# Down projection: three of eight seven-product weight sums per group formed by adding DMAs

## The chip, the core and the metric

One core of one Trainium2 chip runs the kernel. The metric is the device time of one execution in microseconds. Before the change it is 1316.98 us, the median of two runs (1316.85 and 1317.11).

The engines are called as in the profile: PE is TensorE (PEld its weight loads), DVE is VectorE, ACT is ScalarE, POOL is GpSimd, and SP is the engine that only issues transfers here.

## The reference

A block of an encoder with 256 positions of 2048 features in float32: RMSNorm, a combined input projection, a gated branch and a neighbourhood attention, a gated merge, an output projection; then the channel mixer, and a last RMSNorm. The change is in the channel mixer's down projection, `x + a @ w_down`, in which `a` has 256 x 5504 elements and `w_down` 5504 x 2048:

```
h = rms_norm(x, g_norm)
up = h @ w_up
up = (pad[:, :t] * conv_k[0] + pad[:, 1:t + 1] * conv_k[1]
      + pad[:, 2:t + 2] * conv_k[2] + conv_b)
gate, val = jnp.split(up, 2, axis=-1)
return x + (jax.nn.silu(gate) * val) @ w_down
```

## The kernel before

Every float32 operand of a matmul is split in two float32r parts, high and low, and a product is a triple of matmuls: high by high, low by high, high by low (`triple`, L291 to L293). ScalarE makes the high part (L151) and VectorE the low one (L152).

The down projection runs as two groups, each for 1024 output columns. A group walks over the 43 blocks of 128 rows of `w_down`. One such block of 128 x 1024 is a piece: a transfer of 512 KB into one of five raw buffers `wraw` (L126), issued by SP, then the split into `whi` and `wlo`. For a plain piece four triples are multiplied: two blocks of positions (t) by two halves of columns (c). Two pieces make a pair, numbered from 0, so pair q has the pieces 2q and 2q + 1.

In some pairs (`DOWN_QUADS`, seven per group before) the two by two by two block product is done with seven triples in place of eight, with sums of activation blocks and sums of weight blocks (a scheme of the Strassen and Winograd kind). Three helpers prepare such a pair:

- `act_sums` and `act_sums_split` (L295 to L311): one DVE addition of 128 x 512 joins high and low (L298), four of 128 x 128 make the sums (L300 to L303), ACT and DVE split them again (L309, L310).
- `weight_sums` (L313 to L320): four DVE instructions of 128 x 512 on the raw pieces (L316 to L319) make two tiles of 128 x 2 x 512, `t13` and `t24`.
- `weight_sums_split` (L322 to L330): for each of the two tiles an ACT copy (L326) and a DVE subtraction (L327) of 128 x 1024.

The order of all engines is the order of the program, written out by hand: each piece i has a `begin(i)`, which issues loads up to piece i + 4 (`LOAD_AHEAD`), splits pieces up to i + 3 (`SPLIT_AHEAD`), and runs the tasks that were put `at(i)`. For a pair that starts at piece i the activation sums stand at i - 5 and i - 4, the weight sums at i - 3, their split at i - 2. In the products (`run_wide`) the first piece of the pair brings three triples, on raw blocks and one activation sum; the second brings four, on the weight sums.

Each engine takes its instructions in this order. A transfer that SP issues waits on SP's queue until its buffer is free, and holds those behind it. The same is true of POOL's queue, which has few transfers in this stage: the four loads of the last norm's weights (`gfin`, L1272).

Of the kernel before, what the change touches and what calls it, by code (L numbers as in the profile page):

```python
# [8 lines left out]
F32 = mybir.dt.float32  # L9
F32R = mybir.dt.float32r  # L10
AF = mybir.ActivationFunctionType
OP = mybir.AluOpType
# [43 lines left out]
OUT_ORDER = (tuple(range(16)), (0, 1, 6, 7, 2, 3, 10, 11, 4, 5, 8, 9, 12, 13, 14, 15))  # L56
TURN_X2 = (13, 1)
Y_GAP = 224
DOWN_QUADS = ((4, 6, 9, 11, 14, 16, 18), (3, 5, 8, 10, 13, 15, 17))


@with_exitstack
def trunk_kernel(ctx, tc, x, norm_mix, w_in, ln_g, ln_b, w_s, b_s, rpb, w_branch, w_out,
# [41 lines left out]

    raw, split_t = {}, {}
    whole, units = {}, {}
    n_loaded = [0]
    n_split = [0]
    first = {}  # L110

    def load_to(n):
        while n_loaded[0] < min(n, len(pieces)):
            i = n_loaded[0]
            n_loaded[0] += 1
            if i in preload:
                for f in preload[i]:
                    f()
            src, r0, kn, (c0, cn, nb, cs), step = pieces[i]
            w = wpool.tile([128, 2, 512], F32, name="wraw", bufs=LOAD_AHEAD)  # L120
            ld = src.shape[-1]
            if i == 0:
                for k in range(kn):
                    nc.sync.dma_start(w[:, k, :cn], src[r0:r0 + 128, c0 + k * step:c0 + k * step + cn])
            elif nb == 1:
                nc.sync.dma_start(  # L126
                    w[:, :kn, :cn],
                    bass.AP(tensor=src.tensor, offset=src.offset + r0 * ld + c0,
                            ap=[[ld, 128], [step, kn], [1, cn]]))
            else:  # L130
                for b in range(nb):
                    nc.sync.dma_start(
                        w[:, :kn, b * cn:(b + 1) * cn],
                        bass.AP(tensor=src.tensor, offset=src.offset + r0 * ld + c0 + b * cs,
                                ap=[[ld, 128], [step, kn], [1, cn]]))
            raw[i] = w
            if i in whole:
                whole[i] = w
# [30 lines left out]
    def at(i, f):  # L169
        tasks.setdefault(i, []).append(f)  # L170
# [93 lines left out]

    def wide(src, row0, order, c0, acts, quads, room, done, sums=None, odd=None):
        n0 = plan_wide(src, row0, order, c0)
        boxes = {}
        for n, q in enumerate(quads):  # L270
            i = n0 + 2 * q
            own = odd if odd and n % 2 else room
            whole[i] = whole[i + 1] = None
            units[i], units[i + 1] = 1, 2
            b = boxes[q] = {}
            if sums is None:
                b["acts"] = {}
                sum_acts_at(i - 5, i - 4, b["acts"], lambda k=order[2 * q]: ff["ap"][k // 2], room, "s")
            else:
                b["acts"] = sums[order[2 * q]]  # L280
            at(i - 3, lambda i=i, b=b: weight_sums(i, b, room))
            at(i - 2, lambda b=b, own=own: weight_sums_split(b, own))
        return ("wide", n0, order, acts, quads, boxes, done)

# [10 lines left out]
    def act_sums(a, box, room):  # L295
        w = room("f", F32)
        f = w[:, 0].rearrange("p (k t) -> p k t", k=2)
        nc.vector.tensor_add(f, a[:, :, 0, :].bitcast(F32), a[:, :, 1, :].bitcast(F32))  # L298
        s1, s2, s3, s4 = (w[:, 1, n * 128:(n + 1) * 128] for n in range(4))
        nc.vector.tensor_add(s1, f[:, 0, 128:], f[:, 1, 128:])  # L300
        nc.vector.tensor_sub(s3, f[:, 0, :128], f[:, 0, 128:])
        nc.vector.tensor_sub(s2, s1, f[:, 0, :128])
        nc.vector.tensor_sub(s4, f[:, 1, :128], s2)  # L303
        box["w"] = w

    def act_sums_split(box, room, name):
# [6 lines left out]
    def weight_sums(i, box, room):  # L313
        r0, r1 = whole.pop(i), whole.pop(i + 1)
        t13, t24 = room("t13", F32), room("t24", F32)
        nc.vector.tensor_sub(t13[:, 0], r0[:, 1], r0[:, 0])  # L316
        nc.vector.tensor_sub(t24[:, 0], r1[:, 1], t13[:, 0])
        nc.vector.tensor_sub(t13[:, 1], r1[:, 1], r0[:, 1])
        nc.vector.tensor_sub(t24[:, 1], r1[:, 0], t24[:, 0])  # L319
        box["w"] = (t13, t24)  # L320

    def weight_sums_split(box, room):  # L322
        u = []
        for name, t in zip(("13", "24"), box.pop("w")):
            h, l = room("h" + name, F32R), room("l" + name, F32R)
            nc.scalar.activation(h, t, AF.Copy)  # L326
            nc.vector.tensor_sub(l, t, h.bitcast(F32))  # L327
            u.append((h, l))
        box["t"] = {1: [x[:, 0] for x in u[0]], 3: [x[:, 1] for x in u[0]],
                    2: [x[:, 0] for x in u[1]], 4: [x[:, 1] for x in u[1]]}  # L330

    def run_wide(g, tail=0):
        kind, n0, order, acts, quads, boxes, done = g
        n1 = n0 + len(order)
        P = C = None

        def x_of(k, t):
            a = acts(k)
            return a[:, 0, t * 128:(t + 1) * 128], a[:, 1, t * 128:(t + 1) * 128]

        def plain(i, t, c):
            h, l = split_t[i]
            triple(C[t][c], x_of(order[i - n0], t), h[:, c], l[:, c], i == n0, i == n1 - 1)

        for i in range(n0, n1 - tail):
            begin(i)
            q, r = divmod(i - n0, 2)
            if C is None:
                c = [bank() for _ in range(4)]
                C = [c[:2], c[2:]]  # L350
            if q not in quads:
                for t, c in ((0, 0), (0, 1), (1, 0), (1, 1)) if i > 1 else ((0, 0), (1, 0), (0, 1), (1, 1)):
                    plain(i, t, c)
                split_t.pop(i)
                continue
            st, sp = q == quads[0], q == quads[-1]
            k, k1 = order[2 * q:2 * q + 2]
            if r == 0:
                if st:
                    P = [bank() for _ in range(4)]  # L360
                (h0, l0), (h1, l1) = split_t[i], split_t[i + 1]
                triple(P[0], x_of(k, 0), h0[:, 0], l0[:, 0], st, sp)
                triple(C[0][0], x_of(k1, 0), h1[:, 0], l1[:, 0], False, False)
                triple(C[0][1], boxes[q]["acts"]["s"][3], h1[:, 1], l1[:, 1], False, False)
                split_t.pop(i)
                split_t.pop(i + 1)
                continue
            S, W = boxes[q]["acts"]["s"], boxes[q]["t"]
            triple(P[1], S[0], *W[1], st, sp)
            triple(P[3], S[2], *W[3], st, sp)  # L370
            triple(P[2], S[1], *W[2], st, sp)
            triple(C[1][0], x_of(k1, 1), *W[4], False, False)
            if sp:
                done[0](P, i)
        if not tail:
            done[1](C, n1)
            return
        for t in range(NT):
            for c in range(2):
                for i in range(n1 - tail, n1):  # L380
                    if t == 0 and c == 0:
                        begin(i)
                    plain(i, t, c)
                done[1](C, t, c)
# [140 lines left out]
    def post_sums(P, x, spare):  # L525
        p1, p5, p6, p7 = P
        (x11, x12), (x21, x22) = x
        nc.scalar.activation(x11, p1, AF.Copy)
        nc.vector.tensor_add(spare, p6, x11)
        nc.vector.tensor_add(x12, p5, spare)  # L530
        nc.vector.tensor_add(x21, p7, spare)
        nc.vector.tensor_add(x22, p5, x21)

    def add_sums(ps, x):
        for t in range(NT):
            for c in range(2):
                nc.vector.tensor_add(x[t][c], ps[t][c], x[t][c])

    def ev_v_sums(P, i):
        def go():  # L540
# [358 lines left out]
    def ev_sums(j, room):  # L899
        def done(P, i):  # L900
# [5 lines left out]
            def first_half():  # L906
# [1 line left out]
                m["v"], m["u3"], m["w"] = cd[:, 0], cd[:, 1], ab[:, 0]  # L908
                nc.scalar.activation(ab[:, 0], p1, AF.Copy)
                nc.vector.tensor_add(x11, p1, x11)  # L910
                nc.vector.tensor_add(ab[:, 1], p6, ab[:, 0])
                nc.vector.tensor_add(m["v"], p5, ab[:, 1])
                nc.vector.tensor_add(m["u3"], p7, ab[:, 1])
                nc.vector.tensor_add(m["w"], p5, m["u3"])

            def second_half():
                nc.vector.tensor_add(x12, x12, m["v"])
                nc.vector.tensor_add(x21, x21, m["u3"])
                nc.vector.tensor_add(x22, x22, m["w"])

            at(i + 1, first_half)
            at(i + 2, second_half)
# [48 lines left out]
    ff = {}  # L971
# [166 lines left out]
    def down_room(name, dt):  # L1138
        return hpool.tile([128, 2, 512], dt, name=h_room[name])

    g_dn = [wide(w_d, 0, range(NF), g * 1024, lambda k: ff["a"][k], DOWN_QUADS[g], down_room,
                 (ev_sums(2 * g, down_room), ev_down if g == 0 else finish)) for g in range(2)]


    preload[0] = [lambda: load_x(0, 256)]
# [103 lines left out]
    ctx.push(fa_st)  # L1249
    ff["ap"] = [fa.tile([128, min(2, NF - k), 2, T], F32R, name=f"a{k // 2}") for k in range(0, NF, 2)]  # L1250
    ff["a"] = [ff["ap"][k // 2][:, k % 2] for k in range(NF)]
    fc = {}

    def open_conv():
# [54 lines left out]
```

## Time and profile before

| | us |
|---|---|
| median of the two runs | 1316.98 |
| span of the profiled execution | 1314.9 |
| TensorE busy | 1303.3 |
| VectorE busy | 1066.2 |
| ScalarE busy | 764.8 |
| GpSimd busy | 88.3 |
| DMA read from HBM | 253.90 MB, 195 GB/s over the span |

The runs' median lies 2.08 us above the profiled execution's span; the profile lists no other time of that execution. Rows of the order of time read: start, length, engine, line, operation, tiles written and read, shapes, count; behind them in brackets the idle time before and what ended it. In rows of groups the last numbers are the busy time, the mean length of one in ns, and the idle time before. The first group of the down projection begins at about 1080 us and the second at about 1193 us. The tiles of the sums are all named `h` in the profile, since they live in buffers of that name.

### The profile page before, as it was taken

To read this page: it belongs to the slowest core of one execution; us is meant where nothing else is said; L and a number is where in the kernel's file an instruction comes from. 1 tells how busy PE (TensorE), PEld (TensorE's weight loads), DVE (VectorE), ACT (ScalarE), POOL (GpSimd) and SP (SyncE) were. 2 spreads that over 40 slices of the span, in tenths; PEclk is the share of its full clock that TensorE was granted. 3 is DMA by queue.
4 is the path that set the end of the run, shared out by engine and by line. 5 is a ranking of instruction groups with operands and counts; after the bars stand their busy time and mean duration, and the time that the engine had idled before them with its cause. 6 is when DMAs were issued, how large, how long until landed. Compare 5 with 4: busy or idle time off the path is not lost.

```text
span 1314.9 us, 19329 instructions
## 1 busy us (share of the span) xinstructions
PE 1303.3 (99%) x6776; PEld 1112.0 (85%) x6776; DVE 1066.2 (81%) x1625; ACT 764.8 (58%) x1139; POOL 88.3 (7%) x176
## 2 busy tenths in 40 slices
PE   9999999999999999999999999999999999999997
PEld 7888888888888888888888888888888888888885
DVE  7996778667789966986777778787878789999997
ACT  5766476666645644556555555555656556555653
POOL 0004505323000000000000000000000000000000
PEclk9999999999999999999999999999999999999999
DMA  8768656556556657665565665656565656666663
GB/s 305 260 209 235 201 174 201 181 163 194 179 172 209 210 190 241 204 210 163 175 202 182 192 193 182 195 184 193 180 205 177 198 154 226 220 194 206 210 202 119
DMA packets 170577, 259.37 MB, mean 197 GB/s; under 512 B 12664, under 2 KB 124144, under 8 KB 170480
## 3 DMA queue, kind: packets, MB, share of 16 engines
q1 hardware_dynamic: 166448, 250.31, 59.4%
q0 software_dynamic: 3712, 7.30, 2.4%
q8 instruction: 53, 0.87, 0.3%
q10 hardware_dynamic: 320, 0.53, 0.1%
q14 instruction: 44, 0.36, 0.1%
HBM read 253.90 MB, written 2.10 MB: 195 GB/s over the span
## 4 chain that ended last, share of the span: by engine, by line
PE 97%; DVE 1%; ACT 0%; issue 0%; DMA 0%; ACTq 0%; DVEq 0%
PE bank L205 31%; PE bank L209 16%; PE bank L293 12%; PE bank L291 12%; PE bank L292 12%; PE bank L233 5%; PE bank L235 4%; PE bank L234 4%; PE bank L761 1%; DVE wlo L152 0%; PE bank L811 0%; PE bank L503 0%; PE bank L627 0%; PE bank L801 0%; PE bank L892 0%
## 5 line engine op out<-in xcount | busy, mean ns | idle before, releaser
L152 DVE TENSOR_TENSOR wlo<-wraw,whi 128x1024 fp32r<-128x1024 f32 (+1 forms) x472 | 550.3, 1178 | 188.7 <-ACT whi L151 92.0
L151 ACT ACTIVATE whi<-wraw 128x1024 fp32r<-128x1024 f32 (+1 forms) x472 | 472.0, 1015 | 204.7 <-PE bank L292 75.2
L205 PE MATMUL bank<-h,whi 128*128 128x512 f32 x1760 | 426.0, 392 | 0.0
L205 PEld LDWEIGHTS bank<-h,whi 128*128 128x128 f32 x1760 | 321.9, 188 | 62.0 <-DVE ya L631 0.3
L209 PEld LDWEIGHTS bank<-h,wlo 128*128 128x128 f32 x1760 | 225.9, 191 | 8.8
L209 PE MATMUL bank<-h,wlo 128*128 128x256 f32 x1760 | 228.6, 283 | 0.0
L989 ACT ACTIVATE tc<-ta,ck 128x256 f32<-128x256 f32 x86 | 47.1, 594 | 117.1 <-DVE ta L987 117.1
L293 PE MATMUL bank<-wlo,a 128*128 128x512 f32 x260 | 101.5, 390 | 0.2 <-DVE wlo L152 0.2
L292 PE MATMUL bank<-whi,a 128*128 128x512 f32 x260 | 101.2, 389 | 0.0
L291 PE MATMUL bank<-whi,a 128*128 128x512 f32 x260 | 101.2, 389 | 0.0
L291 PE MATMUL bank<-whi,h 128*128 128x512 f32 x204 | 80.3, 393 | 0.0
L292 PE MATMUL bank<-whi,h 128*128 128x512 f32 x204 | 79.5, 390 | 0.0
L293 PE MATMUL bank<-wlo,h 128*128 128x512 f32 x204 | 79.5, 390 | 0.0
L293 PEld LDWEIGHTS bank<-wlo,a 128*128 128x128 f32 x260 | 48.8, 188 | 11.2 <-DVE wlo L152 1.3
L292 PEld LDWEIGHTS bank<-whi,a 128*128 128x128 f32 x260 | 48.8, 188 | 10.3
L291 PEld LDWEIGHTS bank<-whi,a 128*128 128x128 f32 x260 | 48.8, 188 | 10.1
L992 DVE SCALAR_TENSOR_TENSOR tc<-ta,ck,tc 128x255 f32<-128x255 f32 x86 | 41.4, 481 | 14.5 <-ACT tc L989 14.5
L979 ACT ACTIVATE tb<-bank 128x256 f32<-128x256 f32 x86 | 28.3, 385 | 42.2 <-PE bank L205 42.2
L233 PE MATMUL bank<-whi,y 128*128 128x512 f32 x128 | 50.5, 394 | 0.0
L233 PE MATMUL bank<-whi,h 128*128 128x512 f32 x128 | 50.4, 394 | 0.0
L235 PE MATMUL bank<-wlo,h 128*128 128x512 f32 x128 | 49.9, 390 | 0.0
L235 PE MATMUL bank<-wlo,y 128*128 128x512 f32 x128 | 49.9, 390 | 0.0
(299 smaller groups left out, 1744.1 us busy)
## 6 DMA issues: line engine op xcount, KB each, us to landing
wraw<-in_w_up_dram SPq DMA_DIRECT2D x336, 256.0 KB, 3.2
wraw<-in_w_in_dram SPq DMA_DIRECT2D x111, 512.0 KB, 4.5
wraw<-in_w_down_dram SPq DMA_DIRECT2D x86, 512.0 KB, 4.6
wraw<-in_w_in_dram SPq DMA_DIRECT2D x66, 256.0 KB, 3.2
wraw<-in_w_branch_dram SPq DMA_DIRECT2D x32, 512.0 KB, 4.5
wraw<-in_w_out_dram SPq DMA_DIRECT2D x32, 512.0 KB, 3.6
xs<-in_x_dram SPq DMA_DIRECT2D x8, 256.0 KB, 7.6
vw<-y POOLq DMA_DIRECT2D x16, 128.0 KB, 6.9
```

Of the source, the lines that this page charges most:

```text
L151: nc.scalar.activation(h[:, k, :m], w[:, k, :m], AF.Copy)
L152: nc.vector.tensor_sub(l[:, k, :m], w[:, k, :m], h[:, k, :m].bitcast(F32))
L205: nc.tensor.matmul(p, h[:, k - k0, b * 128:(b + 1) * 128], acts(k), start=k == 0, stop=k == nk - 1)
L209: nc.tensor.matmul(p[:, :T], l[:, k - k0, b * 128:(b + 1) * 128], acts(k)[:, 0, :], start=False, stop=False)
L233: nc.tensor.matmul(p, xh, h[:, kk, :m], start=st, stop=False)
L234: nc.tensor.matmul(p, xl, h[:, kk, :m], start=False, stop=False)
L235: nc.tensor.matmul(p, xh, l[:, kk, :m], start=False, stop=sp)
L291: nc.tensor.matmul(p, xh, h, start=st, stop=False)
L292: nc.tensor.matmul(p, xl, h, start=False, stop=False)
L293: nc.tensor.matmul(p, xh, l, start=False, stop=sp)
L989: nc.scalar.activation(v, u, AF.Identity, scale=ck[:, 1, ch:ch + 1], bias=ck[:, 3, ch:ch + 1])
L992: nc.vector.scalar_tensor_tensor(v[:, 1:], u[:, :T - 1], ck[:, 0, ch:ch + 1], v[:, 1:], op0=OP.mult, op1=OP.add)
```

## The change

It does five things.

- The seven-product scheme is written in another form, so that the four weight sums are additions only. This touches the order of the products, the signs in the combinations after them, and the activation sums, which become four DVE instructions in place of five. It holds for all stages that use the scheme.
- Each group of the down projection has eight seven-product pairs in place of seven.
- In three of the eight (pairs 6, 10, 14 of the first group and 5, 9, 13 of the second) the weight sums are not made by VectorE. SP loads `t13` and `t24` straight from `w_down`, and POOL issues three transfers that add to their destination: a second load added to `t13`, half of one added to `t24`, then the first half of `t13` added to both halves of `t24`. They stand at i - 7.
- For such a pair only the first half of piece i is loaded raw.
- `t13` and `t24` of these pairs live in a pool of their own, with one buffer each. The ring memory for POOL's transfers is set to 4096 bytes.

```diff
-DOWN_QUADS = ((4, 6, 9, 11, 14, 16, 18), (3, 5, 8, 10, 13, 15, 17))
+DOWN_QUADS = ((4, 6, 8, 10, 12, 14, 16, 18), (3, 5, 7, 9, 11, 13, 15, 17))
+DOWN_BY_DMA = ((6, 10, 14), (5, 9, 13))
...
+            if i in first_half:
+                kn = 1
...
+            if q in by_dma:
+                at(i - 7, lambda i=i, b=b: weight_sums_dma(i, b, dma_room))
+            else:
+                at(i - 3, lambda i=i, b=b: weight_sums(i, b, room))
             at(i - 2, lambda b=b, own=own: weight_sums_split(b, own))
...
-        nc.vector.tensor_add(s1, f[:, 0, 128:], f[:, 1, 128:])
-        nc.vector.tensor_sub(s3, f[:, 0, :128], f[:, 0, 128:])
-        nc.vector.tensor_sub(s2, s1, f[:, 0, :128])
-        nc.vector.tensor_sub(s4, f[:, 1, :128], s2)
+        nc.vector.tensor_sub(w[:, 1, 0:256].rearrange("p (n t) -> p n t", t=128), blocks[:, 0:4:3],
+                             blocks[:, 1:2].to_broadcast([128, 2, 128]))
+        nc.vector.tensor_add(p2, n1, a11)
+        nc.vector.tensor_sub(s4, a12, p2)
...
-        nc.vector.tensor_sub(t13[:, 0], r0[:, 1], r0[:, 0])
-        nc.vector.tensor_sub(t24[:, 0], r1[:, 1], t13[:, 0])
-        nc.vector.tensor_sub(t13[:, 1], r1[:, 1], r0[:, 1])
-        nc.vector.tensor_sub(t24[:, 1], r1[:, 0], t24[:, 0])
+        nc.vector.tensor_add(t13[:, 0], r0[:, 0], r0[:, 1])
+        nc.vector.tensor_add(t24[:, 1], t13[:, 0], r1[:, 1])
+        nc.vector.tensor_add(t13[:, 1], r0[:, 1], r1[:, 1])
+        nc.vector.tensor_add(t24[:, 0], r1[:, 0], t24[:, 1])
...
+        def part(dr, c, step, n=2):
+            return bass.AP(tensor=src.tensor, offset=src.offset + (r0 + dr) * ld + c0 + c,
+                           ap=[[ld, 128], [step, n], [1, 512]])
+
+        nc.sync.dma_start(t13, part(0, 0, 512))
+        nc.sync.dma_start(t24, part(128, 0, 512))
+        nc.gpsimd.dma_start(t13, part(0, 512, 128 * ld), accum_op=OP.add)
+        nc.gpsimd.dma_start(t24[:, 0:1], part(128, 512, 512, 1), accum_op=OP.add)
+        nc.gpsimd.dma_start(t24, t13[:, 0:1].to_broadcast([128, 2, 512]), accum_op=OP.add)
...
-            triple(P[1], S[0], *W[1], st, sp)
-            triple(P[3], S[2], *W[3], st, sp)
-            triple(P[2], S[1], *W[2], st, sp)
+            triple(P[1], S[1], *W[1], st, sp)
+            triple(P[3], S[0], *W[3], st, sp)
+            triple(P[2], S[2], *W[2], st, sp)
...
-            nc.vector.tensor_add(spare, p6, x11)
+            nc.vector.tensor_sub(spare, x11, p6)
...
-    nc = _bacc.Bacc("TRN2", target_bir_lowering=False, num_devices=1)
+    nc = _bacc.Bacc("TRN2", target_bir_lowering=False, num_devices=1, dynamic_dma_scratch_size=4096)
```

More of the change, by code (lines that the diff above doesn't have):

```diff
@@ L107, in trunk_kernel @@
     whole, units = {}, {}
+    first_half = set()
     n_loaded = [0]
@@ L262, in run_group, with wide @@
             done(ps, b)
-    def wide(src, row0, order, c0, acts, quads, room, done, sums=None, odd=None):
+    def wide(src, row0, order, c0, acts, quads, room, done, sums=None, odd=None, by_dma=(), dma_room=None):
         n0 = plan_wide(src, row0, order, c0)
@@ L272, in wide @@
             own = odd if odd and n % 2 else room
-            whole[i] = whole[i + 1] = None
             units[i], units[i + 1] = 1, 2
+            if q in by_dma:
+                first_half.add(i)
+            else:
+                whole[i] = whole[i + 1] = None
             b = boxes[q] = {}
@@ L280, in wide @@
                 b["acts"] = sums[order[2 * q]]
-            at(i - 3, lambda i=i, b=b: weight_sums(i, b, room))
+            if q in by_dma:
+                at(i - 7, lambda i=i, b=b: weight_sums_dma(i, b, dma_room))
+            else:
+                at(i - 3, lambda i=i, b=b: weight_sums(i, b, room))
             at(i - 2, lambda b=b, own=own: weight_sums_split(b, own))
@@ L298, in act_sums @@
         nc.vector.tensor_add(f, a[:, :, 0, :].bitcast(F32), a[:, :, 1, :].bitcast(F32))
-        s1, s2, s3, s4 = (w[:, 1, n * 128:(n + 1) * 128] for n in range(4))
-        nc.vector.tensor_add(s1, f[:, 0, 128:], f[:, 1, 128:])
-        nc.vector.tensor_sub(s3, f[:, 0, :128], f[:, 0, 128:])
-        nc.vector.tensor_sub(s2, s1, f[:, 0, :128])
-        nc.vector.tensor_sub(s4, f[:, 1, :128], s2)
+        a11, a21, a12, a22 = (w[:, 0, n * 128:(n + 1) * 128] for n in range(4))
+        blocks = w[:, 0].rearrange("p (n t) -> p n t", t=128)
+        nc.vector.tensor_sub(w[:, 1, 0:256].rearrange("p (n t) -> p n t", t=128), blocks[:, 0:4:3],
+                             blocks[:, 1:2].to_broadcast([128, 2, 128]))
+        n1, p2, s4 = (w[:, 1, n * 128:(n + 1) * 128] for n in range(1, 4))
+        nc.vector.tensor_add(p2, n1, a11)
+        nc.vector.tensor_sub(s4, a12, p2)
         box["w"] = w
@@ L315, in weight_sums, with weight_sums_dma @@
         t13, t24 = room("t13", F32), room("t24", F32)
-        nc.vector.tensor_sub(t13[:, 0], r0[:, 1], r0[:, 0])
-        nc.vector.tensor_sub(t24[:, 0], r1[:, 1], t13[:, 0])
-        nc.vector.tensor_sub(t13[:, 1], r1[:, 1], r0[:, 1])
-        nc.vector.tensor_sub(t24[:, 1], r1[:, 0], t24[:, 0])
+        nc.vector.tensor_add(t13[:, 0], r0[:, 0], r0[:, 1])
+        nc.vector.tensor_add(t24[:, 1], t13[:, 0], r1[:, 1])
+        nc.vector.tensor_add(t13[:, 1], r0[:, 1], r1[:, 1])
+        nc.vector.tensor_add(t24[:, 0], r1[:, 0], t24[:, 1])
+        box["w"] = (t13, t24)
+    def weight_sums_dma(i, box, room):
+        src, r0, _, (c0, _, _, _), _ = pieces[i]
+        ld = src.shape[-1]
+        t13, t24 = room("t13", F32), room("t24", F32)
+        def part(dr, c, step, n=2):
[6 more added lines that the diff above has]
+        nc.gpsimd.dma_start(t24, t13[:, 0:1].to_broadcast([128, 2, 512]), accum_op=OP.add)
         box["w"] = (t13, t24)
@@ L329, in weight_sums_split @@
         box["t"] = {1: [x[:, 0] for x in u[0]], 3: [x[:, 1] for x in u[0]],
-                    2: [x[:, 0] for x in u[1]], 4: [x[:, 1] for x in u[1]]}
+                    2: [x[:, 1] for x in u[1]], 4: [x[:, 0] for x in u[1]]}
     def run_wide(g, tail=0):
@@ L536, in add_sums @@
             for c in range(2):
-                nc.vector.tensor_add(x[t][c], ps[t][c], x[t][c])
+                (nc.vector.tensor_sub if c else nc.vector.tensor_add)(x[t][c], ps[t][c], x[t][c])
     def ev_v_sums(P, i):
@@ L910, in first_half @@
                 nc.vector.tensor_add(x11, p1, x11)
-                nc.vector.tensor_add(ab[:, 1], p6, ab[:, 0])
+                nc.vector.tensor_sub(ab[:, 1], ab[:, 0], p6)
                 nc.vector.tensor_add(m["v"], p5, ab[:, 1])
@@ L916, in second_half @@
             def second_half():
-                nc.vector.tensor_add(x12, x12, m["v"])
+                nc.vector.tensor_sub(x12, x12, m["v"])
                 nc.vector.tensor_add(x21, x21, m["u3"])
-                nc.vector.tensor_add(x22, x22, m["w"])
+                nc.vector.tensor_sub(x22, x22, m["w"])
             at(i + 1, first_half)
@@ L1139, in down_room, with more_room @@
         return hpool.tile([128, 2, 512], dt, name=h_room[name])
+    def more_room(name, dt):
+        return ff["more"].tile([128, 2, 512], dt, name=name)
     g_dn = [wide(w_d, 0, range(NF), g * 1024, lambda k: ff["a"][k], DOWN_QUADS[g], down_room,
-                 (ev_sums(2 * g, down_room), ev_down if g == 0 else finish)) for g in range(2)]
+                 (ev_sums(2 * g, down_room), ev_down if g == 0 else finish), by_dma=DOWN_BY_DMA[g], dma_room=more_room)
+            for g in range(2)]
     preload[0] = [lambda: load_x(0, 256)]
@@ L1251, in trunk_kernel @@
     ff["a"] = [ff["ap"][k // 2][:, k % 2] for k in range(NF)]
+    ff["more"], more_st = pool("more")
+    ctx.push(more_st)
     fc = {}
```

## The prediction

> **What bounds the kernel now.** I read the page's first part and its chain first, then busy time by stretch for the down projection, then who made TensorE wait, then the order of time on TensorE, VectorE and the load queue around the pairs that the change touches.
>
> ```profile
> span 1314.9 us, 19329 instructions
> PE 1303.3 (99%) x6776; PEld 1112.0 (85%) x6776; DVE 1066.2 (81%) x1625; ACT 764.8 (58%) x1139; POOL 88.3 (7%) x176
> PE 97%; DVE 1%; ACT 0%; issue 0%; DMA 0%; ACTq 0%; DVEq 0%
> ```
> ```profile
> 1100.00:1176.00 76.00, 76.00 (x337) 62.94 (x336) 73.31 (x104) 42.98 (x49) 0.00 (x0) 1.00 0.62 205
> ```
> ```profile
> PE bank L291 <- ACT h L326: 0.6, 1, 0.6
> PE bank L293 <- DVE wlo L152: 0.2, 1, 0.2
> ```
>
> TensorE is busy for 1303.3 of 1314.9 us and carries 97% of the chain. In the seven-product part of the first down group (second fence, columns PE, PEld, DVE, ACT, POOL, clock, DMA share, GB/s) it never stops, the clock is full, and VectorE works 73.31 of 76 us. In the whole span it waits 0.8 us for ScalarE and VectorE after its start (third fence). So every matmul removed is time won, as long as nothing else begins to arrive late; and VectorE has little room for another pair's sums.
>
> The median of the two runs is 1316.98 us, 2.08 above the profiled span. I carry these 2.08 us along unchanged.
>
> **The change part by part.**
>
> *One more seven-product pair in each group.* It drops one product, three matmuls, per group. The first matmuls that use the sums of pairs 4 and 18 of the first group:
>
> ```profile
> 1104.31 0.39 PE L291 MATMUL bank<-h,h 128*128 128x512 f32 x1
> ...
> 1176.39 0.39 PE L291 MATMUL bank<-h,h 128*128 128x512 f32 x1
> ```
>
> Between them lie 6 seven-product pairs of 21 matmuls and 8 plain ones of 24, 318 in 72.08 us, so 0.2267 us each (the 0.39 is one matmul's own duration; they overlap). Six fewer: 1.36 us, all on the path.
>
> *VectorE.* Here is one full seven-product pair and the plain pair behind it:
>
> ```profile
> 1093.67 0.68 DVE L298 TENSOR_TENSOR h<-a 128x512 f32<-128x512 f32 x1
> ...
> 1095.33 0.42 DVE L486 TENSOR_TENSOR a<-tc,a 128x256 fp32r<-128x256 f32 x1
> 1095.66 1.22 DVE L152 TENSOR_TENSOR wlo<-wraw,whi 128x1024 fp32r<-128x1024 f32 x1
> ...
> 1098.00 0.69 DVE L316 TENSOR_TENSOR h<-wraw 128x512 f32<-128x512 f32 x1
> ...
> 1100.54 1.22 DVE L152 TENSOR_TENSOR wlo<-wraw,whi 128x1024 fp32r<-128x1024 f32 x1
> ...
> 1105.08 0.68 DVE L298 TENSOR_TENSOR h<-a 128x512 f32<-128x512 f32 x1
> ```
>
> From one L298 to the next are 11.41 us, of which 0.33 (L486) belong to the stage before: 11.08 us of VectorE against 45 x 0.2267 = 10.20 of TensorE. That is why before has room for two dense pairs and then needs a longer gap. The four weight sums take 1100.54 - 1098.00 = 2.54 us, so a pair whose sums come by DMA costs 8.54 with its plain neighbour. Alternating, the mean is 9.81, under 10.20: VectorE gains room although there are more pairs.
>
> ```profile
> L301 DVE TENSOR_TENSOR h<-h 128x128 f32<-128x128 f32 x14 | 4.0, 285 | 0.0
> ```
>
> The activation sums lose one instruction (five to four; two of 128x128 become one of 128x256), between nothing and 0.29 us for each set, off the path, in all stages. The sign changes in the combinations swap one addition for one subtraction of the same shape: nothing. Half of one raw piece per DMA pair is no longer loaded; loads are no bound. ScalarE gets the operand splits of one more pair per group, under 4 us, at 42.98 busy of 76.
>
> *The DMA chain.* For each of six pairs SP issues two 512 KB loads, and POOL three adding transfers: A (512 KB into t13), B (256 KB into t24), C (512 KB, t13 into both halves of t24). A waits for t13's load, C for A and B. ScalarE's L326 and VectorE's L327 then split the results. In the changed kernel's instruction order the two loads stand right behind the load of the group's piece i-3, for pair 6 piece 9. Counted back from the load that had to wait for the weight sums of piece 8, that is the row at 1088.24.
>
> ```profile
> 1088.24 0.33 SPq L126 DMA_DIRECT2D wraw<-in_w_down_dram  x1
> ```
> ```profile
> 1115.87 0.39 PE L291 MATMUL bank<-h,h 128*128 128x512 f32 x1
> ...
> 1131.51 0.39 PE L291 MATMUL bank<-h,h 128*128 128x512 f32 x1
> ```
> ```profile
> 1126.09 2.36 DVE L327 TENSOR_TENSOR h<-h,h 128x1024 fp32r<-128x1024 f32 x2
> ```
> ```profile
> L327 DVE TENSOR_TENSOR h<-h,h 128x1024 fp32r<-128x1024 f32 x28 | 32.9, 1218 | 0.0
> L326 ACT ACTIVATE h<-h 128x1024 fp32r<-128x1024 f32 x28 | 28.2, 1054 | 21.3 <-DVE h L318 21.2
> wraw<-in_w_down_dram SPq DMA_DIRECT2D x86, 512.0 KB, 4.6
> ```
>
> Pair 6 stands at the same place in both kernels, and TensorE first uses a product of t24 there at 1115.87. Less 1.22 (L327) and 1.05 (L326), t24 must be complete at 1113.60. The load goes out at 1088.57: 25.0 us, less 4.6 for the load, leave 20.4 us for A + B + C, where B counts only what it adds behind A.
>
> The later DMA pairs have less. t13 and t24 have one buffer each, so the next load waits for the previous pair's L327, and two DMA pairs stand 90 matmuls, 20.4 us, apart. VectorE can be ahead of the need: pair 9 of before had its L327s done at 1128.45, 3.06 before 1131.51. Over the two gaps of a group that makes 21.9 us each. The t13 load may start 1.13 (one L327's step) before the second L327 ends; then 4.6 for the load, A + B + C, 1.05 and 1.22. So A + B + C may take 16.2 us; beyond that everything is late by the difference, in pairs 10 and 14, then 9 and 13.
>
> No row shows an adding transfer. The nearest are plain ones from POOL's queue: four of 512 KB issued together, and two of 256 KB by themselves.
>
> ```profile
> L927 POOL DMA_DIRECT2D x<-in_x_dram x4: 704/711/728, 512.7 to 514.8; - x4
> DMA to landing us min/median/max: 6.4/7.8/10.4
> ```
> ```profile
> L1272 POOL DMA_DIRECT2D gfin<-in_norm_final_dram x2: 537/538/539, 1210.1 to 1214.1; - x2
> DMA to landing us min/median/max: 3.6/4.0/4.4
> ```
>
> Taking the shortest as the first and the longest as the last, the four landed between 519.1 and 525.2: 2.0 us for each further 512 KB, 1.0 for 256. So A and C lie between 3.6 + 1.0 = 4.6 and 10.4. I take 6.4, the first of the four, as the row of the same queue, size and source beside the same kind of loads, and 1.0 for B: 13.8 us, 2.4 less than the later pairs allow.
>
> Does the volume fit? Each 20.4 us gain 1.05 MB of loads less 0.26 (39 GB/s) and 1.31 MB of adds (64, or 128 if each byte counts twice), on 205: 308 to 372 GB/s. The core has moved more:
>
> ```profile
> 16.00:20.00 4.00, 4.00 (x23) 3.31 (x22) 3.86 (x10) 2.89 (x5) 0.00 (x0) 1.00 1.06 409
> ```
>
> It fits, with little to spare in the second case.
>
> *Waits added and what stands behind them.* SP's t13 load waits for the previous L327; behind it are the raw loads of pieces i-2 on, which would go at most two L327s (2.36) earlier, and run five pieces (some 12 us) ahead of their use at 4.6 each: nothing. POOL's adds wait for loads; behind them is gfin, used a group later: nothing. ScalarE's L326 waits for C; behind it are the splits of the next pieces, so a late C stops the whole feed: this one counts, and is the sum above.
>
> *Smaller ring for POOL's transfers.* This touches the transfers of the attention. The first mask is done at 141.73 and first used at 180.5; 38 us cover it.
>
> ```profile
> 141.22 0.51 POOL L726 TENSOR_SCALAR_AFFINE_SELECT bias<-bias 64x256 f32<-64x256 f32 x1
> ```
> ```profile
> L769 DVE SCALAR_TENSOR_TENSOR sc<-bank,bias x32: 407/422/429, 180.5 to 347.5; 64x256 f32<-64x256 f32 x32
> ```
>
> Sum: 1314.9 - 1.36 + 2.08 = 1315.6 us.
>
> **The rivals.**
>
> *Adding costs twice.* An adding transfer must read its destination as well as its source, so its moving part could count double: A = C = 8.4, B = 2.0, together 18.8. That is 2.6 late in each of four pairs, 10.4 us: 1326.0. For it speaks that nothing in the trace shows adding for free; against it, that 6.4 was taken in a crowd and the quiet gfin rows are far shorter. [...]
>
> *The buffer loop runs over, slower by more than 2%.* With the raw loads at 205 GB/s beside them, A and C could each take the 10.4 us of the last of the four, with B 2.0: 22.8. Then the first DMA pair is 2.4 late and the others 6.6, 15.6 in a group: 1346.8. It passes 2% when A + B + C is 22.2 us. Against it: that 10.4 had three transfers ahead of it in its queue, and here there is at most one.
>
> *POOL starved by the smaller ring.* The masks would have to come 38 us later; below that the time is the forecast's. If the first alone came 48 late, some 10 us would be added: 1326.
>
> *More than the matmuls.* If the 0.8 us of waits also went: 1314.8. Over 2% faster (26 us) is out of reach, as TensorE's whole idle time is 11.6.
>
> **How the numbers follow.** Chains hidden 0.46; late within 2% (the first rival, anything from 1 to 26 us) 0.36; loop over 2% 0.14; ring 0.03; over 2% faster 0.01. The 2% (about what a measurement of this kernel can tell from no change) gives faster 0.01, same 0.85, slower 0.14. The forecast's own range is 1314.4 to 1318. The whole range goes from 1314.4 (waits gone, and the runs' 0.13 either way) to 1338, which holds the lateness up to A + B + C near 21, and leaves out the loop and the worst of the first rival.
>
> **What would show it.** Right: TensorE's waits in the down stage stay under 2 us, A and C land within 8 us, L326 on t24 starts without waiting for a DMA, and VectorE's share falls from 73.31 in 76. Wrong: L326 waits for a DMA in the second and third DMA pair and TensorE stops at the product behind it (adding costs more), or already in the first (the loop is over); waits of L769 for POOL would show the ring; raw splits (L151) that wait for a DMA would show that the volume does not fit.

## The result and the profile after

The changed kernel takes 1347.49 us, the median of two runs (1346.31 and 1348.66), against 1316.98: 1.0233 times before, with a 95% interval of 1.0213 to 1.0252. It is slower by 30.5 us where 1315.6 had been forecast, and outside the range. The profiled span is 1344.5 us, 29.6 more than before.

The page of the changed kernel, its first part and its chain:

```profile
span 1344.5 us, 19387 instructions
PE 1315.7 (98%) x6770; PEld 1116.3 (83%) x6770; DVE 1064.8 (79%) x1601; ACT 768.5 (57%) x1145; POOL 108.4 (8%) x194
PE 84%; DMA 9%; DVE 4%; issue 2%; ACT 1%; POOL 0%; ACTq 0%; SPq 0%; DVEq 0%; POOLq 0%
```

Six matmuls fewer, and yet TensorE is busy 12.4 us longer. The chain now runs through transfers for 9% of the span. Who made TensorE wait, over the whole span but for its start:

```profile
PE bank L301 <- ACT h L354: 15.2, 6, 5.1
PE bank L303 <- DVE wlo L156: 2.2, 4, 1.1
PE bank L303 <- DVE h L355: 0.7, 2, 0.5
```

That is 18.1 us where before had 0.8. L354 and L355 are the splits of the weight sums (L326 and L327 before). ScalarE's L354 in turn waits for transfer C. Of the 15.2 us, 14.6 are five stops at the products of DMA pairs: 3.26, 2.79 and 5.12 us in the first group, 2.70 and 0.71 in the second. The first DMA pair of the second group makes none. The busy time by stretch shows a second loss (columns as before: PE, PEld, DVE, ACT, POOL, granted clock, DMA share, GB/s):

```profile
1100.00:1176.00 76.00, 64.56 (x254) 50.30 (x254) 52.67 (x69) 33.67 (x39) 8.95 (x9) 0.91 0.84 232
1176.00:1220.00 44.00, 44.00 (x188) 36.15 (x187) 42.27 (x56) 22.80 (x26) 0.54 (x1) 0.96 0.68 224
1220.00:1300.00 80.00, 75.45 (x314) 60.09 (x312) 66.03 (x92) 42.71 (x56) 10.47 (x11) 0.96 0.86 246
```

In the first stretch 254 matmuls are done where before did 337, and the clock, 1.00 before, is 0.91. Busy time times the missing clock is 64.56 x 0.09 + 44.00 x 0.04 + 75.45 x 0.04 = 10.6 us. So 17.3 us of added waits (18.1 less 0.8), 10.6 of clock, less 1.4 for the matmuls, make 26.5 of the 29.6 us. The clock's part is an estimate from shares rounded to two digits, and the other 3 us are not resolved by these rows.

Here is the chain of the first DMA pair (pair 6): SP's two loads, POOL's A, B and C, ScalarE's two splits, and TensorE.

```profile
1089.42 0.42 SPq L343 DMA_DIRECT2D t<-in_w_down_dram  x1
1090.15 0.33 SPq L344 DMA_DIRECT2D t<-in_w_down_dram  x1
```
```profile
1096.55 1.21 POOL L345 DMA_DIRECT2D t<-in_w_down_dram  x1 [581.39 <-DMA t<-in_w_down_dram]
1098.16 0.91 POOL L346 DMA_DIRECT2D t<-in_w_down_dram  x1 [0.39 <-issue]
1108.04 1.21 POOL L347 DMA_DIRECT2D t<-t  x1 [8.98 <-DMA t<-in_w_down_dram]
...
1121.87 1.23 POOL L345 DMA_DIRECT2D t<-in_w_down_dram  x1 [11.44 <-DVE h L308]
```
```profile
1108.67 1.05 ACT L354 ACTIVATE h<-t 128x1024 fp32r<-128x1024 f32 x1
1117.77 1.06 ACT L354 ACTIVATE h<-t 128x1024 fp32r<-128x1024 f32 x1 [8.05 <-DMA t<-t]
```
```profile
1118.88 0.79 PE L301 MATMUL bank<-h,h 128*128 128x512 f32 x1 [3.26 <-ACT h L354]
```

From t13's load to A's issue are 7.1 us (4.6 had been put in), from A to C 11.5, from C to the split 9.7. A + B + C is 21.2 us; 13.8 had been forecast and 20.4 was allowed. Over the six pairs it lies between 18.2 and 23.9. By the prediction's times A would have started at 1088.57 + 4.6 = 1093.17; it started 3.4 us later. So the larger part of this first delay lies ahead of the adds, but with 13.8 us for A + B + C the pair would still have been in time. TensorE stops for 3.26 us, and its next matmul takes 0.79 us in place of 0.39.

The second pair's A goes out only at 1121.87, 25.3 us after the first one's, where two such pairs stand 20.4 apart. The profile names a VectorE row behind it, but that had long been done; A waits for t13's load, and this load goes out only when C of the first pair, which reads the one buffer of t13, has landed. SP's queue, and who it waited for:

```profile
1117.74 0.33 SPq L343 DMA_DIRECT2D t<-in_w_down_dram  x1
```
```profile
SPq L343 <- DMA t<-t: 25.0, 4, 8.4
```

### The profile page after: what moved, and what is told of

Same layout as the page of the kernel before. It is cut to its first block, busy times and chain, and to the rows that moved or that the text cites. A ratio compares the mean times of both kernels' runs of the same rounds, so it can differ in the third digit from the quotient of the medians.

```text
span 1344.5 us, 19387 instructions
## 1 busy us (share of the span) xinstructions
PE 1315.7 (98%) x6770; PEld 1116.3 (83%) x6770; DVE 1064.8 (79%) x1601; ACT 768.5 (57%) x1145; POOL 108.4 (8%) x194
## 4 chain that ended last, share of the span: by engine, by line
PE 84%; DMA 9%; DVE 4%; issue 2%; ACT 1%; POOL 0%; ACTq 0%; SPq 0%; DVEq 0%; POOLq 0%
PE bank L209 30%; PE bank L213 16%; PE bank L301 8%; PE bank L303 8%; PE bank L302 7%; DMA t<-in_w_down_dram 5%; PE bank L237 4%; PE bank L239 4%; PE bank L238 4%; DMA t<-t 4%; DVE wlo L156 2%; ACT h L354 1%; PE bank L789 1%; PE bank L839 0%; DVE h L355 0%
## 5 line engine op out<-in xcount | busy, mean ns | idle before, releaser
L156 DVE TENSOR_TENSOR wlo<-wraw,whi 128x1024 fp32r<-128x1024 f32 (+1 forms) x472 | 549.5, 1176 | 187.7 <-ACT whi L155 92.9
L303 PE MATMUL bank<-wlo,a 128*128 128x512 f32 x248 | 98.8, 399 | 2.2 <-DVE wlo L156 2.2
L301 PE MATMUL bank<-whi,a 128*128 128x512 f32 x248 | 99.0, 399 | 0.0
L302 PE MATMUL bank<-whi,a 128*128 128x512 f32 x248 | 98.5, 397 | 0.0
L303 PE MATMUL bank<-wlo,h 128*128 128x512 f32 x206 | 80.2, 390 | 0.0
L354 ACT ACTIVATE h<-t 128x1024 fp32r<-128x1024 f32 x32 | 32.7, 1051 | 52.8 <-DMA t<-t 37.3
L345 POOL DMA_DIRECT2D t<-in_w_down_dram x6 | 7.2, 1197 | 681.0 <-DMA t<-in_w_down_dram 581.4
```

The source lines that it names most:

```text
L156: nc.vector.tensor_sub(l[:, k, :m], w[:, k, :m], h[:, k, :m].bitcast(F32))
L301: nc.tensor.matmul(p, xh, h, start=st, stop=False)
L302: nc.tensor.matmul(p, xl, h, start=False, stop=False)
L303: nc.tensor.matmul(p, xh, l, start=False, stop=sp)
```

## The experiments

All times are medians with their ratio to before on the same chip, whose median there was 1316.4 to 1316.9 us.

**The rest of the change alone.**

```diff
-DOWN_QUADS = ((4, 6, 8, 10, 12, 14, 16, 18), (3, 5, 7, 9, 11, 13, 15, 17))
-DOWN_BY_DMA = ((6, 10, 14), (5, 9, 13))
+DOWN_QUADS = ((4, 6, 9, 11, 14, 16, 18), (3, 5, 8, 10, 13, 15, 17))
+DOWN_BY_DMA = ((), ())
```

> The changed kernel with seven pairs per group as before and none of them by DMA: only the rewritten signs and orders and the smaller ring are left. Loop theory (the adding transfers take too long for the one buffer of t13 and t24, and all the loss comes from there): 1317 us, like before, no wait of TensorE over 1 us in the down stage. Rival (the rewritten sums or the ring cost time): a good part of the 30 us stays, 1325 or more, and the profile shows it outside the down stage.

Measured: 1316.88 us, 0.9999 (0.9990 to 1.0009). The rewritten sums and the ring of 4096 bytes cost nothing. The whole loss lies in the eighth pair and the transfers.

**The eighth pair without transfers** (`DOWN_BY_DMA` empty, eight pairs).

> Eight pairs per group, all weight sums on VectorE. Loop theory: eight dense pairs ask VectorE for 11.0 us where TensorE needs 10.2 for each pair and its neighbour, so over seven such stretches it falls some 5 us behind, less its lead of about 3: a few small waits, 1316 to 1321 us, far under the changed kernel's 1347. Rival (the denser pairs are themselves the loss): 1335 or more.

Measured: 1327.43 us, 1.0082 (1.0067 to 1.0098), 10.5 us over before, more than was expected of it. TensorE waits in short pieces for VectorE:

```profile
PE bank L303 <- DVE wlo L156: 8.1, 13, 1.2
```

So VectorE cannot carry eight pairs; and the changed kernel is 20 us slower than this, so the pairs' density is not its loss.

**The transfers with no engine reading their result** (seven pairs, none of them by DMA).

```diff
+    for g in range(2):
+        for q in BESIDE[g]:
+            i = g_dn[g][1] + 2 * q
+            at(i - 7, lambda i=i: weight_sums_dma(i, {}, more_room))
     run_wide(g_dn[0])
```

> Seven pairs per group with all sums on VectorE, and the transfers of the six DMA pairs issued beside them into tiles that nobody reads. Loop theory: nothing waits for them, 1317 to 1319 us. Rival (the added volume on the DMA engines slows the raw loads): raw splits wait for loads, 1325 us or more. The adding transfers should take 8 to 10 us each here too.

Measured: 1325.26 us, 1.0072 (1.0054 to 1.0089): the rival's number. ScalarE's raw splits wait for loads:

```profile
ACT whi L156 <- DMA wraw<-in_w_down_dram: 15.3, 10, 4.7
```
```profile
1100.00:1176.00 76.00, 72.96 (x318) 59.10 (x317) 68.09 (x90) 39.93 (x46) 8.99 (x9) 1.00 0.91 276
```

The DMA engines are 91% busy there (62% before), and the clock is 1.00. The 8.4 us are not shown to be the price of the volume, though. The raw halves are loaded here as well, 0.26 MB more for each pair than in the changed kernel. And one thing still waits for the transfers: t13's next load waits on SP's queue for C, which reads t13's one buffer, and holds the raw loads behind it.

```profile
SPq L344 <- DMA t<-t: 19.0, 3, 8.1
```

The three longest waits of the raw splits, 3.48, 4.72 and 3.85 us, end 7 to 10 us after these three holds. The early start below has two buffers, no such hold, and nearly the same volume; there the raw splits wait 0.6 us in all.

**Plain copies in place of adds.**

```diff
-        nc.gpsimd.dma_start(t13, part(0, 512, 128 * ld), accum_op=OP.add)
+        nc.gpsimd.dma_start(t13, part(0, 512, 128 * ld))
...
-        nc.gpsimd.dma_start(t24, t13[:, 0:1].to_broadcast([128, 2, 512]), accum_op=OP.add)
+        nc.gpsimd.dma_start(t24, t13[:, 0:1].to_broadcast([128, 2, 512]))
```

> The changed kernel with plain copies in place of the adding transfers (the weight sums of the DMA pairs are left out; same bytes, same queue, same waits). If adding itself costs (the destination is read too), A and C fall from about 10 and 8 us to about 6 each, the loop fits, and the time is 1316 to 1322. If the time of a transfer from this queue beside the raw loads is the cost, they stay at 8 to 10 us and the time within 5 us of 1347.

Measured: 1318.26 us, 1.0015 (1.0006 to 1.0024). This kernel leaves the sums of these pairs out. With the same bytes, queue and order, 29 of the 30.5 us are gone. Transfer A of the changed kernel, then of this one (the first row's numbers are POOL's time to issue it, in ns):

```profile
L345 POOL DMA_DIRECT2D t<-in_w_down_dram x6: 1165/1197/1228, 1096.6 to 1268.8; - x6
...
DMA to landing us min/median/max: 7.9/10.0/10.4
```
```profile
L345 POOL DMA_DIRECT2D t<-in_w_down_dram x6: 708/712/721, 1096.0 to 1244.1; - x6
...
DMA to landing us min/median/max: 5.6/6.9/8.1
```

POOL's queue by packets, MB and share of 16 engines' span, of before, of the changed kernel, and of this one:

```profile
q0 software_dynamic: 3712, 7.30, 2.4%
```
```profile
q0 software_dynamic: 7840, 15.16, 5.4%
```
```profile
q0 software_dynamic: 5920, 15.16, 3.9%
```

For the same added 7.86 MB the adds take 0.054 x 1344.5 - 0.024 x 1314.9 = 41.0 us of engine time and the copies 0.039 x 1315.9 - 31.6 = 19.7: from these rounded shares an add costs the engines 2.1 times what a copy does. Why is not shown: it could be the second read that the prediction's rival argued with, and it could be the packets, which are also half as large (1.9 KB against 3.6).

**The start and the buffers.** Two kernels: two buffers each for t13 and t24, with the chain still at i - 7; and the same with the chain at i - 11. Both have a ring of 2048 bytes, for room.

```diff
-        return ff["more"].tile([128, 2, 512], dt, name=name)
+        return ff["more"].tile([128, 2, 512], dt, name=name, bufs=2)
...
-                at(i - 7, lambda i=i, b=b: weight_sums_dma(i, b, dma_room))
+                at(i - 11, lambda i=i, b=b: weight_sums_dma(i, b, dma_room))
```

The early start first:

> The changed kernel with two buffers each for t13 and t24, and the DMA chain issued at i - 11 in place of i - 7 (the ring is 2048 bytes to make room). Loop theory: A + B + C, 21 us as measured, now has about 30, so no split waits for an add any more and the clock stays full; what is left is the volume, as with the transfers issued beside (8 us over before, less 1.4 for the matmuls): 1320 to 1325 us. Rival (the chain is late for another reason, or the volume is the larger part): 1335 or more, with splits waiting for raw loads.

Measured: 1321.74 us, 1.0040 (1.0025 to 1.0055), the expected number: 25.7 of the 30.5 us gone though the adds are as slow as ever (A 10.8 us). So the loss lies in when the sums are done, not in the adds as such. Splits still wait for C (10.9 us in four pairs), but no stop of TensorE is longer than 1.1 us, and the clock stays at 1.00 from 1080 to 1300 us.

```profile
PE bank L303 <- DVE wlo L156: 3.1, 5, 1.1
...
PE bank L301 <- ACT h L354: 0.8, 2, 0.6
PE bank L303 <- DVE h L355: 0.7, 2, 0.5
```

The expectation put what is left down to the volume, as with the transfers issued beside. But the raw splits hardly wait for loads here, with the DMA engines 87% busy:

```profile
ACT whi L155 <- DMA wraw<-in_w_down_dram: 0.6, 2, 0.3
```
```profile
1100.00:1176.00 76.00, 74.12 (x324) 60.10 (x323) 69.51 (x94) 41.96 (x49) 8.96 (x9) 1.00 0.87 265
```

What is left shows as short waits for VectorE; what makes VectorE late there was not tested.

One DMA pair per group, in which no buffer is waited for:

```diff
-DOWN_BY_DMA = ((6, 10, 14), (5, 9, 13))
+DOWN_BY_DMA = ((10,), (9,))
```

> Eight pairs per group, but only one of them by DMA (pair 10 of the first group, 9 of the second), so no DMA pair follows another in its buffers. Loop theory: A + B + C of 21 us start from the place of the first pair, which allowed 20.4 and was 3 us late there; here VectorE, with seven full pairs, is itself behind by up to 5 us, so the add is hardly late: 1319 to 1325 us, with the waits of TensorE for VectorE. Rival (each DMA pair costs its 5 us by itself): 1327 plus 5 for each of two, less what VectorE saves: 1330 or more.

Measured: 1331.04 us, 1.0107 (1.0092 to 1.0122), with a wide spread (1327.33 to 1333.28). It contradicts the loop theory in its first form. TensorE stops for 2.48 and 1.00 us at the splits of these two pairs, though nothing holds their buffers (the other 0.6 of the 4.1 us below lies in another stage, as in before); most of the rest is VectorE, which now has seven full pairs.

```profile
PE bank L303 <- DVE wlo L156: 6.4, 11, 1.2
PE bank L301 <- ACT h L354: 4.1, 3, 2.5
```

That called for the two buffers at the old start:

> The changed kernel with two buffers each for t13 and t24 and the chain still issued at i - 7 (ring 2048 bytes): the loop through the buffers is gone, the place of the start is not moved. If the loop made the lateness: 1321 to 1324 us, as with the early start. If the start at i - 7 is late by itself (one DMA pair alone waited 1.0 and 2.5 us for its add), every DMA pair stays some 2 to 4 us late, stops of under 3 us without loss of clock: 1328 to 1338.

Measured: 1336.90 us, 1.0158 (1.0135 to 1.0180), again with a wide spread (1333.87 to 1340.92). Taken in this order, the loop through the buffers is worth 10.6 us of the loss (1347.5 to 1336.9), and the start at i - 7 another 15.2 (1336.9 to 1321.7). Contrary to its expectation not every DMA pair was late by 2 to 4 us: there were stops of 1.46 and 0.99, and one long one of 6.24.

**Less by DMA.** Two ways to shorten the chain: C as one addition on VectorE; and only t13 by an add, with t24 as two additions on VectorE.

```diff
-        nc.gpsimd.dma_start(t24, t13[:, 0:1].to_broadcast([128, 2, 512]), accum_op=OP.add)
...
+            nc.vector.tensor_add(t24, t24, t13[:, 0:1].to_broadcast([128, 2, 512]))
```

> The changed kernel with C done by VectorE (one addition of 128x1024 in front of the split) and A and B by DMA. Loop theory: A + B take 12 to 13 us of the 16 allowed, so nothing is late: 1316 to 1321 us, with small waits for VectorE. Rival (volume): splits wait for raw loads, 1323 or more.

Measured: 1321.14 us, 1.0037 (1.0024 to 1.0050).

```diff
-        nc.sync.dma_start(t24, part(128, 0, 512))
...
-        nc.gpsimd.dma_start(t24[:, 0:1], part(128, 512, 512, 1), accum_op=OP.add)
-        nc.gpsimd.dma_start(t24, t13[:, 0:1].to_broadcast([128, 2, 512]), accum_op=OP.add)
...
+        nc.vector.tensor_add(t24[:, 1], t13[:, 0], r1[:, 1])
+        nc.vector.tensor_add(t24[:, 0], r1[:, 0], t24[:, 1])
```

> The changed kernel with only t13 of the DMA pairs formed by an add (its load and A); t24 is two additions of 128x512 on VectorE in its old place. The volume of adds falls from 1.31 to 0.52 MB a pair and the chain to one load and A, some 15 us. If lateness and volume were all, nothing is late, and the six matmuls show: 1315.5 to 1317. If VectorE's load decides (11.1 and 9.8 us by turns against 10.2), short waits eat the gain: 1317 to 1321.

Measured: 1319.61 us, 1.0024 (1.0015 to 1.0034). No split of the weight sums waits for a transfer in either, and the lateness is gone; the waits that are left are for VectorE. Of the second:

```profile
PE bank L305 <- DVE wlo L156: 2.8, 6, 0.9
```

Both stay above before: the 1.4 us of the matmuls are smaller than the short waits.

**The sums on POOL's own arithmetic.**

```diff
-                at(i - 7, lambda i=i, b=b: weight_sums_dma(i, b, dma_room))
+                at(i - 3, lambda i=i, b=b: weight_sums(i, b, dma_room, nc.gpsimd))
```

> Eight pairs per group; in the pairs 6, 10, 14 and 5, 9, 13 the four weight sums are additions on POOL in place of the DMA chain, no added transfer. No volume and no chain: if POOL does the four in under 5 us, the split at i - 2 is not late and the time is 1315.5 to 1318. If POOL takes 8 us or more, or VectorE slows beside it, the split waits as it did for the adds: 1322 or more.

Measured: 1337.57 us, 1.0162 (1.0145 to 1.0179). POOL's first four additions take 8.0 us from start to end, but ScalarE's splits wait for POOL only 5.4 us in the whole stage. TensorE waits 12.5 us for VectorE's raw splits. The last two of the four, then VectorE beside them and just after:

```profile
1105.82 2.27 POOL L327 TENSOR_TENSOR t<-wraw 128x512 f32<-128x512 f32 x1
1108.05 1.74 POOL L328 TENSOR_TENSOR t<-wraw,t 128x512 f32<-128x512 f32 x1
```
```profile
1104.63 2.31 DVE L156 TENSOR_TENSOR wlo<-wraw,whi 128x1024 fp32r<-128x1024 f32 x1
1106.86 1.77 DVE L305 TENSOR_TENSOR h<-a 128x512 f32<-128x512 f32 x1
...
1110.63 1.22 DVE L156 TENSOR_TENSOR wlo<-wraw,whi 128x1024 fp32r<-128x1024 f32 x1
1111.77 0.68 DVE L319 TENSOR_TENSOR h<-h,h 128x512 fp32r<-128x512 f32 x1
```

The same subtraction (L156) takes 2.31 us beside POOL and 1.22 after it. The adding transfers had no such effect on VectorE's own instructions: from 1095 to 1176 us in the changed kernel this subtraction has a mean of 1.22 us, as in before.

**Stops of TensorE without any transfer.** The kernel before, with an activation block rewritten n times by ScalarE, with the same values, ahead of four pieces.

```diff
+    def rewrite(k):
+        for _ in range(2):
+            nc.scalar.activation(ff["a"][k][:, 0, :], ff["a"][k][:, 0, :].bitcast(F32), AF.Copy)
+
+    for g, k in ((0, 1), (0, 39), (1, 1), (1, 38)):
+        at(g_dn[g][1] + k, lambda k=k: rewrite(k))
```

> The kernel before with four stops of TensorE put into the down stage, each by two rewrites of an activation block on ScalarE (same values) that the next piece waits for. Each stop should be about 2 us. Clock theory (a stop of some 3 us or more costs the full clock for the next 4 to 5 us, shorter ones don't): the time grows by about the stops alone, 6 to 9 us, and the granted clock stays 1.00. Rival (any stop costs clock): 12 us or more.

Measured: 1332.04 us, 1.0117 (1.0102 to 1.0132). One stop came out at 7.29 us, since ScalarE was still busy with the stage before; the other three at 1.67. They add to 12.3 us, and the time grew by 15.4. The expected 6 to 9 us missed that long stop, after which the clock was 0.52 over the window from 1090 to 1095 us.

> The same with ten rewrites at each of the four places, stops of about 5 us and no added transfer. Clock theory: the granted clock falls to about 0.5 for some 4 us after each stop and each costs 2 us more than the stop itself: 20 us of stops and 8 of clock, 26 to 32 us in all. Rival (the low clock of the changed kernel came with its DMA traffic): the clock stays 1.00 and the time grows by the stops, 18 to 22 us.

Measured: 1351.57 us, 1.0268 (1.0251 to 1.0285), with stops of 10.87 and three times 5.26 us, 26.6 in all; the time grew by 34.9. Two 5 us windows: one of the kernel with two rewrites, behind a stop of 1.67 us, and one of the kernel with ten, at the end of a stop of 5.26.

```profile
1195.00:1200.00 5.00, 5.00 (x24) 4.14 (x23) 4.07 (x5) 1.89 (x2) 0.00 (x0) 1.00 0.75 274
```
```profile
1200.00:1205.00 5.00, 4.35 (x10) 3.47 (x11) 1.37 (x3) 0.56 (x2) 0.00 (x0) 0.50 0.47 169
```

After the short stop 24 matmuls fit into 5 us. After the long one the granted clock is 0.50 for the next 4.35 us, and only 10 fit. The four long stops cost (34.9 - 26.6) / 4 = 2.1 us each beyond their length, without a single added transfer; and the early start, with all the adding transfers and no long stop, kept its clock at 1.00. The low clock of the changed kernel thus follows from its stops and needs no other cause.

A length of 3 us, which these two expectations and that of the two buffers put in for such a stop, is shown by no run: some shorter ones were enough. The first stop below is the changed kernel's of 2.70 us, with the slow stretch behind it; the second is one of 1.85 us with the sums on POOL, and the stretch behind that.

```profile
1265.46 0.79 PE L301 MATMUL bank<-h,h 128*128 128x512 f32 x1 [2.70 <-ACT h L354]
```
```profile
1265.22:1272.05 6.83, 6.55 (x15) 4.67 (x16) 6.50 (x10) 4.18 (x6) 1.75 (x2) 0.50 0.77 217
```
```profile
1111.91 0.50 PE L300 MATMUL bank<-wlo,a 128*128 128x512 f32 x1 [1.85 <-DVE wlo L156]
```
```profile
1112.42:1115.83 3.41, 3.41 (x9) 2.68 (x9) 3.41 (x5) 3.41 (x5) 0.00 (x0) 0.50 0.79 238
```

Two more stops of the same kernel, of 1.89 and 1.91 us, cost no clock; with the two buffers a stop of 1.46 us did, with a second one of 0.53 close behind it.

## Why the prediction was wrong

*Right:* TensorE carries the time. That each matmul removed is worth 0.227 us was not seen, as every kernel here with eight pairs had some waits. VectorE is relieved by the DMA pairs (with plain copies in their place the time is 1318.3, with all sums on VectorE 1327.4). The smaller ring and the rewritten sums cost nothing, and no engine waited for what stands behind the adds on POOL's queue. The wait on ScalarE's L326 was named as the one that counts, and it came already in the first pair, which the prediction had named as a sign of being wrong.

*The step that failed* is the size of A + B + C: "I take 6.4, the first of the four, as the row of the same queue, size and source beside the same kind of loads, and 1.0 for B: 13.8 us". The first pair measured 21.2 us, from A's issue at 1096.55 to the split at 1117.77. All six lie between 18.2 and 23.9. A plain copy there takes 6.9 us, so the row was a good one for a copy; an add takes 10.0. The rival "adding costs twice" was right that the cost doubles, as the engine time of the queue shows (41.0 us against 19.7), though its own sum, 18.8 us, was still low. Its reason, the second read, was the author's argument; no run shows that this read sets the time.

*The load ahead of it* had been put at 4.6 us, the median beside 62% busy engines. Two loads issued together, in a stretch with all the others, took 7.1 us to A's issue.

*"Does the volume fit?"* In the changed kernel no raw split waits for a load, and in the early start they wait 0.6 us, so the answer held as far as these runs go.

*"Waits added"* had t13's load wait for the previous split and put what stands behind it at nothing. It waits for C, which reads t13, up to 8.4 us at a time, with the raw loads behind it. In the changed kernel no raw split waited for that; in the kernel where no engine reads the sums raw splits waited 15.3 us for loads, longest behind these holds.

*The allowance* for the later pairs looked only at the buffers. One pair alone, with free buffers, was late as well: from the place i - 7 the chain's length is too much by itself. The buffers are worth 10.6 us and the place 15.2.

*What was missing* was the price of a stop. The rivals counted lateness one to one. The four stops of 2.70 to 5.12 us cost some 2 to 3 us more each, an estimated 10.6 us over the stage. The rival "the buffer loop runs over" gave 1346.8 us, close to the 1347.5 measured, partly by chance: its 22.8 us for A + B + C lie among those measured, but it had more lateness (31.2 us) than the 17.3 of added waits, and no clock.

No version here beats before. The best with eight pairs, 1318.3 with plain copies, computes no sums in those pairs and is still above 1316.9: eight pairs have 1.4 us to win, and VectorE's short waits take it.

## What to carry to other kernels

Price a transfer that adds to its destination apart from a copy: here it took 10.0 us where a copy of the same 512 KB took 6.9, and the adds took 41.0 us of engine time where the copies took 19.7. For a chain of dependent transfers add each step at the rate of the busy stretch, and compare the sum with the distance from its issue to its use as well as with the time until its buffers come round. A tile that a transfer still read held up the next load into it by up to 8.4 us here, and with that the whole queue of this load. When TensorE is the bound, price a stop of 2.5 us or more at its length plus 2 to 3 us of slow clock (here 2.1 each for one stop of 10.87 and three of 5.26, and an estimated 10.6 in all for the four of 2.70 to 5.12), and expect that a shorter one can cost clock too, as that of 1.85 us did.

## What the runs showed of the hardware

- In the down stage of these runs the granted clock fell to 0.50 after every stop of 2.48 us or more, with matmuls of 0.63 us in place of 0.39, and it was 1.00 over the windows behind three stops of 1.67. Below 2.48 the length alone does not decide: 3.41 us at 0.50 followed a stop of 1.85 us, matmuls of 0.63 us also followed two of 1.46 and 0.53 close together, and none followed stops of 1.89 and 1.91.
- With the sums on POOL, VectorE's subtraction L156 of 128x1024 took 2.31 us beside POOL's additions and 1.22 after them, and its subtraction in the split of VectorE's own weight sums, of the same size, took 1.60 on average (1.22 in before).
- POOL took 1.20 us to issue an add of 512 KB and 0.71 to issue a copy (transfer A, medians of six); the adds moved in packets of 1.9 KB (7.86 MB in 4128), the copies in packets of 3.6 KB (in 2208).
